# Last part of W2 gated by columns, x written into the PSUM banks ahead of its products, last norm read from PSUM

## The chip, the cores and the metric

The kernel runs on one core of one Trainium2 chip. The metric is the device time in microseconds (us) of one execution. A profiled execution has a span (first to last event in its trace) that is a little shorter than its device time. In the profile PE is TensorE's products, PEld its weight loads, DVE is VectorE, ACT is ScalarE, POOL is GpSimd, SP is SyncE, which issues the DMAs.

## The reference, cut to what matters

Two layers of a diffusion trunk over 640 tokens (128 context tokens and 512 latent tokens) with 1024 features. The change is in the second half of the last layer, whose MLP ends in a gated sum and a LayerNorm:

```python
def _layer_norm(x, g, b, eps=1e-5):
    mu = jnp.mean(xf, axis=-1, keepdims=True)
    var = jnp.mean(jnp.square(xf - mu), axis=-1, keepdims=True)
    y = (xf - mu) * lax.rsqrt(var + eps) * g + b

def _block(x, mod, mixer, g, b, w1, w2):
    sh1, sc1, gt1, sh2, sc2, gt2 = jnp.split(mod, 6, axis=-1)
    ...
    hf = x * (1 + sc2) + sh2
    ff = jnp.square(jax.nn.relu(hf @ w1)) @ w2
    x = _layer_norm(ALPHA * x + gt2 * ff, g[1], b[1])
```

The gate gt2 is one row of 1024 numbers for the context tokens and another for all latent tokens. So for the latent tokens gt2 * (h @ w2) may also be computed as h @ (w2 with its columns multiplied by gt2).

## The kernel before

The 640 tokens are five tiles t = 0 to 4 of 128; t = 0 is the context. x is kept in SBUF as two halves a = 0, 1 of 512 columns for each t. Every product of a weight W is made of three fp32r products: each weight unit `wraw` (128 rows, 1024 columns, 512 KB) is loaded by DMA into one of three slots (`NRAW`), then split by `Unit.split` into `whi`, a rounded copy made by ACT, and `wlo`, the rest made by DVE. Five split units fit at once (`NSPL`). An activation is split in the same way (`ghi`, `glo`).

The MLP goes in eight groups g of 512 hidden features. For g = 0 to 6, DVE collects the products of W2 in `y`; at g = 6, POOL multiplies `y` by the gate row and DVE adds it to ALPHA * x. For the last group, g = 7, `mlp_block(t, nh)` makes the product of tile t and column half nh in a PSUM bank `fps` (12 products of 512 columns over two units of W2), and `gated` has DVE multiply the bank by the gate row (`tmp`) and add it to x. After both halves of a tile, `norm` runs: DVE's `bn_stats` on both halves and `bn_aggr`, a square root on ACT, four small DVE operations that give `r` and `nmr`, and in the last layer the result itself. There a column range is done either by ACT (scale and shift by r and nmr), then two POOL operations (times the row ln_g, plus the row ln_b), or by two DVE operations (`stt`); `cut` says how many columns of tile t go the first way. Each finished range is written to `y` by a DMA from SP.

The order in which the engines get their instructions is set by a planner in the kernel (`class Order`): it advances a modelled clock, and where several steps could go next it takes the one that its own costs make ready first. Each engine's queue then runs strictly in that order; an instruction that waits holds all those behind it. `use(key)` makes sure that the units of a piece of W2 are split before its products, and `background` loads and splits units ahead when a slot is free. In the profile nearly all instructions have the line of a helper: L379 for DVE, ACT and POOL, L468 for products, L452 for DMAs, so that they are told apart by their tiles.

Of the kernel before, what the change touches and what calls it, by code (L numbers as in the profile page):

```python
# [13 lines left out]
ALU = mybir.AluOpType  # L14
# [392 lines left out]
def trunk_kernel(ctx: ExitStack, tc: tile.TileContext, io: dict, layers: int = 2, stop: str = ""):  # L407
# [105 lines left out]
    class Unit:  # L513


        def __init__(self, src, kt, n, own=False):
            self.src, self.kt, self.n, self.own = src, kt, n, own

        def load(self):
            tot = self.kt * self.n  # L520
# [4 lines left out]
        def split(self):  # L525
            tot = self.kt * self.n
            raw, self.raw = self.raw, None
            if self.own:

                self.hs, self.ls = [], []  # L530
                for k in range(0, self.kt, 2):
                    c = slice(k * self.n, min(k + 2, self.kt) * self.n)
                    w = c.stop - c.start
                    h, l_ = slot("whs")[:, :w].bitcast(F32R), slot("wls")[:, :w].bitcast(F32R)
                    act.copy(h, raw[:, c])
                    vec_tt(l_, raw[:, c], h.bitcast(F32), op=ALU.subtract)
# [12 lines left out]
            self.lo = lo[:, :tot].rearrange("p (k n) -> p k n", k=self.kt)  # L549
# [109 lines left out]
            yield 0.0  # L659

    done = set()
    pieces = {}
    units = []
    rank = {}
# [17 lines left out]
    for l in range(layers):  # L682
        if l == 1:
            add_piece((1, "SKVG"), [Unit(io["w_odd0"][:, 288 * a:288 * b], b - a, 288)
                                    for a, b in ((0, 3), (3, 6), (6, 8))])
            for n, kname in enumerate(ODD[1:]):
                add_piece((1, kname), [Unit(io["w_odd"][n, u], 4, 256) for u in range(2)])
        for h in range(2):
            for n in range(4):
                add_piece((l, "O", h, n), [Unit(io["w_out"][l, h, n], 4, 256)])  # L690
        for g in range(8):
            for n in range(2):
                add_piece((l, "1", 2 * g + n), [Unit(io["w_1"][l, 2 * g + n, u], 4, 256, g + n == 0) for u in range(2)])
            for n in range(2):
                add_piece((l, "2", g, n), [Unit(io["w_2"][l, g, n, u], 2, 512) for u in range(2)])
    pos = [0, 0, 0]
    mod_steps = []
    for c in range(6 if layers > 1 else 0):
# [230 lines left out]
    def norm(t, rows, ft, A, B, final, key, xd=None):  # L929
# [19 lines left out]
        time = order.step[:]  # L949
        if final:  # L950

            cut = (1024, 1024, 1024, 1024, 256)[t]
            for a, c0, c1 in ((0, 0, 256), (0, 256, 512), (1, 0, 512)) if t == NT - 1 else ((0, 0, 512), (1, 0, 512)):
                c, far = slice(c0, c1), 512 * a + c1 <= cut
                x, g, b = X[t][a][:, c], rows[0][a][:, c], rows[1][a][:, c]
# [7 lines left out]
                load(io["y"][t * P:(t + 1) * P, 512 * a + c.start:512 * a + c.stop], x)  # L963
            return
        def update():
            for a in range(2):
# [959 lines left out]
    def layer(l, ft, xd):  # L1926
# [34 lines left out]
        for g in range(8):  # L1961
# [14 lines left out]
            else:  # L1976
                if g == 6:
                    need_mods(l, (5,))
                    rows = gate_rows(l, 1)
                for f in range(4):  # L1980
                    sp = pss("ff") if f < 2 else None
                    for half in range(2):
# [9 lines left out]
                        squared(two(sp), *[two2(x) for x in (*parts[f], slot("relu2")[:, :TOK])])  # L1992

            def mlp_block(t, nh):
                w = use((l, "2", g, nh), (l, "2", g, 0) if last else None)
# [19 lines left out]
            else:  # L2015
                ln = ln_rows(l, 1)
                ft_n = A = B = None
                if not last_layer:
# [2 lines left out]
                    A, B = norm_cols(l, 1)  # L2021
                    ft_n = FT("h")
                xd = [[dram.tile([P, 512], F32, name=nm("xd")) for _ in range(2)] for _ in range(NT)]
                for t in range(NT):
                    for nh in range(2):
                        order.gemm(lambda: mlp_block(t, nh))
                    order.spawn(norm(t, ln, ft_n, A, B, last_layer, ("h", l, t), xd[t]))
        if last_layer:
            order.drain(lambda: not order.chains)
            return None, None  # L2030
# [114 lines left out]
```

## Time and profile before

| | us |
|---|---|
| median of three runs | 1635.65 (1634.84 to 1637.54) |
| the profiled execution | 1635.63 |
| its span | 1633.8 |
| PE busy | 1570.0 (96%) |
| DVE, ACT, POOL busy | 1018.0, 610.4, 524.7 |

The profiled execution is as long as the median. PE is busy nearly all the way, so a time is mostly a sum of products; the stretch that the change touches is the last 45 us, from the last group's first product with W2 at 1589.57 us of the span to its end.

### The profile page before, as it was taken

What the parts mean: (1) busy time and instruction counts of PE and PEld (TensorE: products, weight loads), DVE (VectorE), ACT (ScalarE), POOL (GpSimd) and SP (SyncE); (2) the same over time, 40 slices, a digit from 0 to 9 for tenths busy, and PEclk for the clock granted to TensorE, in tenths of its full rate; (3) what the DMA queues carried; (4) which work ended last, traced back from release to release, by engine and by line L of the source; (5) the groups of instructions that cost most, each with busy time, mean ns of one, the idle gap of its engine ahead of it and who ended that gap; (6) DMA issues with size and microseconds to landing.
All of it is one profiled execution on the core that took longest, in us unless ns stands there. A gap on an engine that the chain in (4) does not pass through costs nothing.

```text
span 1633.8 us, 28517 instructions
## 1 busy us (share of the span) xinstructions
PE 1570.0 (96%) x11345; PEld 1421.7 (87%) x11345; DVE 1018.0 (62%) x1943; ACT 610.4 (37%) x1279; POOL 524.7 (32%) x451
## 2 busy tenths in 40 slices
PE   7999999999999999999999998889999999999996
PEld 4998999999889889988988887779989988998994
DVE  3776662676477677676786788777824444444457
ACT  2554443336323222222255555553633222322321
POOL 2110000012467777777537347231200010011226
PEclk9999999999999999999999999999999999999998
DMA  9633334341444444463324101114212222223121
GB/s 333 204 119 118 102 98 162 130 134 52 139 136 143 148 139 152 147 182 114 112 68 139 61 28 39 56 43 155 79 52 78 78 78 72 71 75 113 58 78 65
DMA packets 89844, 177.75 MB, mean 109 GB/s; under 512 B 23648, under 2 KB 30832, under 8 KB 89712
## 3 DMA queue, kind: packets, MB, share of 16 engines
q1 hardware_dynamic: 89712, 175.94, 33.6%
q8 instruction: 89, 1.46, 0.4%
q14 instruction: 43, 0.35, 0.1%
HBM read 169.40 MB, written 6.50 MB: 108 GB/s over the span
## 4 chain that ended last, share of the span: by engine, by line
PE 80%; DVE 6%; ACT 5%; POOL 4%; DMA 2%; issue 2%; SPq 0%; POOLq 0%; DVEq 0%; ACTq 0%
PE ff L468 25%; PE fps L468 24%; PE proj L468 11%; PE ops L468 6%; PE fproj L468 3%; ACT h L379 1%; PE early L468 1%; DMA wmod<-in_w_mod 1%; POOL x L379 1%; PE sd L468 1%; PE po L468 1%; DVE wlo L379 1%; POOL y L379 1%; PE odp L468 1%; PE gl L468 1%
## 5 line engine op out<-in xcount | busy, mean ns | idle before, releaser
L468 PE MATMUL ff<-hh,whi 128*128 128x320 f32 (+2 forms) x960 | 297.2, 310 | 0.0
L468 PE MATMUL ff<-hh,wlo 128*128 128x320 f32 (+2 forms) x960 | 296.5, 309 | 0.1
L468 PE MATMUL ff<-hl,whi 128*128 128x320 f32 (+2 forms) x960 | 296.4, 309 | 0.0
L379 ACT CAST whi<-wraw 128x1024 fp32r<-128x1024 f32 (+1 forms) x183 | 189.3, 1045 | 285.4 <-PE fps L468 250.5
L379 DVE TENSOR_TENSOR wlo<-wraw,whi 128x1024 fp32r<-128x1024 f32 (+1 forms) x183 | 244.2, 1339 | 68.8 <-ACT whi L379 68.6
L468 PE MATMUL fps<-wlo,ghi 128*128 128x512 f32 (+1 forms) x648 | 253.9, 392 | 2.0 <-DVE wlo L379 2.0
L468 PE MATMUL fps<-whi,ghi 128*128 128x512 f32 (+1 forms) x648 | 254.5, 393 | 0.0
L468 PE MATMUL fps<-whi,glo 128*128 128x512 f32 (+1 forms) x648 | 253.5, 391 | 0.0
L379 POOL TENSOR_TENSOR x<-x,lnrow 128x512 f32<-128x512 f32 (+1 forms) x78 | 110.4, 1429 | 347.9 <-DVE y L379 216.7
L468 PEld LDWEIGHTS ff<-hh,whi 128*128 128x128 f32 x960 | 180.2, 188 | 3.1 <-issue 2.1
L379 DVE TENSOR_TENSOR relu<-relu 128x320 f32<-128x320 f32 (+3 forms) x100 | 64.1, 641 | 189.5 <-ACT ghi L379 185.9
L468 PEld LDWEIGHTS ff<-hl,whi 128*128 128x128 f32 x960 | 180.2, 188 | 0.6
L468 PEld LDWEIGHTS ff<-hh,wlo 128*128 128x128 f32 x960 | 180.2, 188 | 0.4 <-DVE wlo L379 0.4
L379 ACT ACTIVATE relu<-ff 128x320 f32<-128x320 f32 (+3 forms) x100 | 51.4, 514 | 295.2 <-PE ff L468 295.2
L379 DVE TENSOR_TENSOR y<-fps,y 128x512 f32<-128x512 f32 x120 | 82.6, 689 | 117.8 <-PE fps L468 117.7
L468 PEld LDWEIGHTS fps<-wlo,ghi 128*128 128x128 f32 x648 | 121.8, 188 | 29.9 <-DVE wlo L379 2.9
L468 PEld LDWEIGHTS fps<-whi,ghi 128*128 128x128 f32 x648 | 121.6, 188 | 29.6 <-issue 2.5
L468 PEld LDWEIGHTS fps<-whi,glo 128*128 128x128 f32 x648 | 121.7, 188 | 28.0
L379 POOL TENSOR_SCALAR wmod<-wmod,cs 128x512 f32<-128x512 f32 x84 | 95.2, 1134 | 124.1 <-DVE moda L379 108.5
L379 POOL TENSOR_TENSOR moda<-moda,wmod 128x512 f32<-128x512 f32 x84 | 123.5, 1470 | 6.2
L468 PE MATMUL ops<-wlo,cath 128*128 128x256 f32 x320 | 90.2, 282 | 2.2 <-DVE wlo L379 2.2
L468 PE MATMUL proj<-whi,hh 128*128 128x256 f32 (+1 forms) x280 | 83.9, 300 | 8.6 <-DVE sg L379 5.7
(295 smaller groups left out, 3372.2 us busy)
## 6 DMA issues: line engine op xcount, KB each, us to landing
wraw<-in_w SPq DMA_DIRECT2D x128, 512.0 KB
wmod<-in_w_mod SPq DMA_DIRECT2D x128, 256.0 KB
wmodp<-in_w_mod SPq DMA_DIRECT2D x64, 256.0 KB
wraw<-in_w_even SPq DMA_DIRECT2D x24, 512.0 KB
wraw<-in_w_out SPq DMA_DIRECT2D x16, 512.0 KB
wraw<-in_w_odd SPq DMA_DIRECT2D x16, 512.0 KB
gate<-mrow SPq DMA_DIRECT2D x16, 256.0 KB
xT<-in_xT SPq DMA_DIRECT2D x8, 320.0 KB
```

What stands on the lines that cost most here:

```text
L379: i = f(*a, **k)
L468: nc.tensor.matmul(o, a, b, **kw)
```

## The change

For the tiles t = 1 to 4 of the last layer's last group, four things are done otherwise. First, the four units of W2 for g = 7 are loaded once more (piece `"gated"`), and POOL multiplies each by the latent gate row, two operations of 128x512 per unit, before ACT and DVE split it. Tile 0 still goes the old way, through the ungated units and `gated`. Second, `preload` opens the PSUM bank of a block one block ahead: one product that starts the bank, and an ACT copy of x (128x512) into that bank over the result of the product; the 12 products of `whole_block` then add to what stands there. Third, the DVE multiply and add of `gated` are gone for these tiles, and `norm` reads the banks in place of x. Fourth, in the last norm half of the columns of t = 1 to 3 go to DVE's two operations (`cut` is 512 in place of 1024), and tile 4's last half is done in two ranges of 256.

```diff
@@ Unit.split
+            if self.gate is not None:
+                for k in range(self.kt):
+                    c = slice(k * self.n, (k + 1) * self.n)
+                    pool.tensor_tensor(raw[:, c], raw[:, c], last_gates[self.gate][:, :self.n], op=ALU.mult)
...
@@ the list of units
+    for n in range(2):
+        add_piece(("gated", n), [Unit(io["w_2"][layers - 1, 7, n, u], 2, 512, gate=n) for u in range(2)])
...
@@ norm
-            dve.bn_stats(st[:, i, :], X[t][a][:, c0:c1])
+            dve.bn_stats(st[:, i, :], source(a, c0, c1))
...
-            cut = (1024, 1024, 1024, 1024, 256)[t]
+            cut = (1024, 512, 512, 512, 256)[t]
...
-                    act.activation(x, x, AF.Identity, scale=r, bias=nmr)
+                    act.activation(x, y, AF.Identity, scale=r, bias=nmr)
...
-                    stt(x, x, mv[:, 0:1], g, op0=ALU.subtract, op1=ALU.mult)
+                    stt(x, y, mv[:, 0:1], g, op0=ALU.subtract, op1=ALU.mult)
...
@@ layer
+                def preload():
+                    if todo:
+                        t, a, c0, c1 = todo.pop(0)
+                        ps = (acc if t in (1, 3) or c0 else pss)("out", True)
+                        banks.setdefault(t, {})[a, c0, c1] = ps
+
+                        hv = parts[0][0]
+                        mm(ps[:, :c1 - c0], hv[:, :128], hv[:, :c1 - c0], start=True, stop=False)
+                        act.copy(ps[:, :c1 - c0], X[t][a][:, c0:c1])
+
+                def whole_block(t, a, c0, c1):
+                    preload()
+                    w = use(("gated", a), ("gated", 0))
+                    c, n, ps = tcol(t), slice(c0, c1), banks[t][a, c0, c1][:, :c1 - c0]
+                    for f in range(4):
+                        hv, lv = parts[f]
+                        mm(ps, hv[:, c], w.hi(f, n), start=False, stop=False)
+                        mm(ps, hv[:, c], w.lo(f, n), start=False, stop=False)
+                        mm(ps, lv[:, c], w.hi(f, n), start=False, stop=(f == 3))
```

What the planner makes of it is seen in the queues. On POOL, behind the last product of `y` and the gate (`y_14079`), there stood before only the last norm. x_12786 and x_13014 are the halves of tile 0, x_12831 and x_13048 those of tile 1:

```order
L379 TENSOR_TENSOR y_14079<-y_14079,gate_16313 128x512
L379 TENSOR_TENSOR x_12786<-x_12786,lnrow_17011 128x512
L379 TENSOR_TENSOR x_13014<-x_13014,lnrow_17013 128x512
L379 TENSOR_TENSOR x_12786<-x_12786,lnrow_17015 128x512
L379 TENSOR_TENSOR x_13014<-x_13014,lnrow_17017 128x512
L379 TENSOR_TENSOR x_12831<-x_12831,lnrow_17011 128x512
```

Now, at the same place on POOL, wraw_16951 and wraw_16983 are the gated units of the left half (the first and the second unit), wraw_17078 and wraw_17131 those of the right half (the third and the fourth):

```order
L379 TENSOR_TENSOR y_14079<-y_14079,gate_16313 128x512
L379 TENSOR_TENSOR wraw_16951<-wraw_16951,gate_16311 128x512 x2
L379 TENSOR_TENSOR wraw_16983<-wraw_16983,gate_16311 128x512 x2
L379 TENSOR_TENSOR wraw_17078<-wraw_17078,gate_16313 128x512 x2
L379 TENSOR_TENSOR x_12786<-x_12786,lnrow_17015 128x512
L379 TENSOR_TENSOR x_13014<-x_13014,lnrow_17017 128x512
L379 TENSOR_TENSOR x_12786<-x_12786,lnrow_17019 128x512
L379 TENSOR_TENSOR x_13014<-x_13014,lnrow_17021 128x512
L379 TENSOR_TENSOR wraw_17131<-wraw_17131,gate_16313 128x512 x2
L379 TENSOR_TENSOR x_12831<-x_12831,lnrow_17015 128x512
```

Three units are gated ahead of tile 0's norm and the fourth behind it; tiles 1 to 3 have two POOL operations each in place of four.

On ACT, behind the split of the last ungated unit (whi_17049), there now stand copies of x into banks (out_17053 and out_17080 for tile 1, out_17133 and out_17177 for tile 2), the splits of the gated units (whi_17074, whi_17085, whi_17127, whi_17138, in the order of POOL above), and tile 0's norm between them:

```order
L379 CAST whi_17049<-wraw_16852 128x1024
L379 COPY out_17053<-x_12831 128x512
L379 COPY out_17080<-x_13048 128x512
L379 CAST whi_17074<-wraw_16951 128x1024
L379 CAST whi_17085<-wraw_16983 128x1024
L379 COPY out_17133<-x_12879 128x512
L379 ACTIVATE sq_17107<-mv_17102,eps_t 128x1
L379 ACTIVATE x_12786<-x_12786,nmr_17110,r_17109 128x512
L379 ACTIVATE x_13014<-x_13014,nmr_17110,r_17109 128x512
L379 CAST whi_17127<-wraw_17078 128x1024
L379 CAST whi_17138<-wraw_17131 128x1024
L379 COPY out_17177<-x_13082 128x512
```

Before, the same split of the last ungated unit was followed by the norms alone, one square root and two scalings for each tile:

```order
L379 CAST whi_17045<-wraw_16852 128x1024
L379 ACTIVATE sq_17087<-mv_17082,eps_t 128x1
L379 ACTIVATE x_12786<-x_12786,nmr_17090,r_17089 128x512
L379 ACTIVATE x_13014<-x_13014,nmr_17090,r_17089 128x512
L379 ACTIVATE sq_17143<-mv_17138,eps_t 128x1
```

On DVE, behind the sum of tile 0's right half (x_13014), the queue is now the rest of the left half's gated units, the whole norm of tile 0 up to nmr, the rest of the right half's units, and then tile 1's norm, which reads the banks:

```order
L379 TENSOR_TENSOR x_13014<-x_13014,tmp_17069 128x512
L379 TENSOR_TENSOR wlo_17075<-wraw_16951,whi_17074 128x1024
L379 TENSOR_TENSOR wlo_17086<-wraw_16983,whi_17085 128x1024
L379 BN_STATS bn_17101<-x_12786 128x6
L379 BN_STATS bn_17101<-x_13014 128x6
L379 BN_AGGR mv_17102<-bn_17101 128x2
L379 TENSOR_SCALAR veh_17106<-mv_17102 128x1
L379 RECIPROCAL sq_17107<-sq_17107 128x1
L379 TENSOR_SCALAR q_17108<-sq_17107,veh_17106 128x1
L379 TENSOR_SCALAR r_17109<-q_17108,sq_17107 128x1
L379 TENSOR_SCALAR nmr_17110<-mv_17102,r_17109 128x1
L379 TENSOR_TENSOR wlo_17128<-wraw_17078,whi_17127 128x1024
```

The two sums of tile 1's halves, which stood among these rows before, are gone. On PE the product that opens out_17080 stands directly behind tile 0's right half, and the one that opens out_17133 behind tile 1's left half. Up to the last group's products the queues of PE, DVE, ACT and POOL are as before; on SP two of the four added loads stand ahead of the last norm's rows, and two behind.

## Rows read from the trace of the kernel before

**Rows 1.** The page's first part, the engines over the whole span.
```profile
span 1633.8 us, 28517 instructions
PE 1570.0 (96%) x11345; PEld 1421.7 (87%) x11345; DVE 1018.0 (62%) x1943; ACT 610.4 (37%) x1279; POOL 524.7 (32%) x451
```

**Rows 2.** The chain that ended last, 1500 us on: start us, length us, what.
```profile
1533.82 27.74 PE fps L468 x120
...
1595.17 12.53 PE fps L468 x53
...
1611.63 18.63 POOL x L379 x13
```

**Rows 3.** Timeline of PE: start us, length us, operation [idle before it, released by].
```profile
1595.17 0.50 PE L468 MATMUL fps<-wlo,ghi 128*128 128x512 f32 x1 [1.02 <-DVE wlo L379]
...
1596.19 0.40 PE L468 MATMUL fps<-whi,glo 128*128 128x512 f32 x1
...
1618.55 0.28 PE L468 MATMUL fps<-whi,glo 128*128 128x256 f32 x1
```

**Rows 4.** Timeline of DVE, columns as for PE.
```profile
1597.96 0.69 DVE L379 BATCH_NORM_STATS2 bn<-x 128x6 f32<-128x512 f32 x1
...
1603.51 0.27 DVE L379 TENSOR_SCALAR q<-sq,veh 128x1 f32<-128x1 f32 x1
...
1604.06 0.21 DVE L379 TENSOR_SCALAR nmr<-mv,r 128x1 f32<-128x1 f32 x1
...
1618.87 0.42 DVE L379 TENSOR_TENSOR tmp<-fps,gate 128x256 f32<-128x256 f32 x1
...
1622.68 0.26 DVE L379 BATCH_NORM_AGGREGATE mv<-bn 128x2 f32<-128x24 f32 x1
1622.98 0.74 DVE L379 SCALAR_TENSOR_TENSOR x<-x,mv,lnrow 128x256 f32<-128x256 f32 x1
...
1625.99 2.47 DVE L379 SCALAR_TENSOR_TENSOR x<-x,r,lnrow 128x256 f32<-128x256 f32 x2
```

**Rows 5.** Timeline of ACT, columns as for PE.
```profile
1590.67 1.04 ACT L379 CAST whi<-wraw 128x1024 fp32r<-128x1024 f32 x1
1601.44 0.30 ACT L379 ACTIVATE sq<-mv,eps_t 128x1 f32<-128x1 f32 x1 [9.72 <-DVE mv L379]
1604.31 1.52 ACT L379 ACTIVATE x<-x,nmr,r 128x512 f32<-128x512 f32 x2 [2.58 <-DVE nmr L379]
```

**Rows 6.** ACT's groups over the whole span: count, busy us, mean ns, idle before.
```profile
L379 ACT CAST hh<-h 128x512 fp32r<-128x512 f32 x30 | 18.9, 629 | 0.5
L379 ACT COPY y<-fps 128x512 f32<-128x512 f32 x20 | 11.8, 588 | 35.0 <-PE fps L468 35.0
```

**Rows 7.** Timeline of POOL, columns as for PE.
```profile
1541.08 2.15 POOL L379 TENSOR_TENSOR y<-y,gate 128x512 f32<-128x512 f32 x1 [1.46 <-issue]
1544.63 1.29 POOL L379 TENSOR_TENSOR y<-y,gate 128x512 f32<-128x512 f32 x1 [1.40 <-DVE y L379]
...
1611.63 19.43 POOL L379 TENSOR_TENSOR x<-x,lnrow 128x512 f32<-128x512 f32 x14 [0.46 <-ACT x L379]
```

**Rows 8.** Timeline of DVE at two splits in earlier stretches.
```profile
1522.89 1.22 DVE L379 TENSOR_TENSOR wlo<-wraw,whi 128x1024 fp32r<-128x1024 f32 x1
...
1540.86 1.22 DVE L379 TENSOR_TENSOR wlo<-wraw,whi 128x1024 fp32r<-128x1024 f32 x1
```

**Rows 9.** Windows: stretch, length, engines' busy us (instructions), granted clock, DMA share, GB/s.
```profile
1526.50:1527.00 0.50, 0.50 (x5) 0.50 (x5) 0.00 (x0) 0.12 (x1) 0.00 (x0) 1.00 0.43 172
1527.00:1527.50 0.50, 0.50 (x6) 0.50 (x4) 0.00 (x0) 0.47 (x2) 0.00 (x0) 1.00 0.08 8
```

**Rows 10.** PE after a long wait in the middle of the kernel, timeline.
```profile
1059.27 0.55 PE L468 MATMUL proj<-whi,hh 128*128 128x256 f32 x1 [5.66 <-DVE sg L379]
```

**Rows 11.** Windows around that wait, columns as in the other windows.
```profile
1060.00:1063.00 3.00, 3.00 (x16) 3.00 (x15) 0.37 (x2) 3.00 (x9) 2.28 (x3) 0.50 0.00 0
1063.00:1064.00 1.00, 1.00 (x9) 1.00 (x7) 0.11 (x1) 0.07 (x1) 1.00 (x2) 0.76 0.00 0
```

More of the change, by code (lines that the diff above doesn't have):

```diff
@@ L513, in trunk_kernel, with __init__ @@
     class Unit:
-        def __init__(self, src, kt, n, own=False):
-            self.src, self.kt, self.n, self.own = src, kt, n, own
+        def __init__(self, src, kt, n, own=False, gate=None):
+            self.src, self.kt, self.n, self.own, self.gate = src, kt, n, own, gate
         def load(self):
@@ L661, in trunk_kernel @@
     done = set()
+    last_gates = []
     pieces = {}
@@ L927, in summed, with norm, source @@
             stt(x, x, ALPHA, y, op0=ALU.mult, op1=ALU.add)
-    def norm(t, rows, ft, A, B, final, key, xd=None):
+    def norm(t, rows, ft, A, B, final, key, xd=None, banks=None):
+        def source(a, c0, c1):
+            for (h, b0, b1), ps in (banks or {}).items():
+                if h == a and b0 <= c0 and c1 <= b1:
+                    return ps[:, c0 - b0:c1 - b0]
+            return X[t][a][:, c0:c1]
         cuts = [(0, 0, 512), (1, 0, 512)] if t < NT - 1 else [(0, 0, 256), (0, 256, 512), (1, 0, 256), (1, 256, 512)]
@@ L950, in norm @@
         if final:
-            cut = (1024, 1024, 1024, 1024, 256)[t]
-            for a, c0, c1 in ((0, 0, 256), (0, 256, 512), (1, 0, 512)) if t == NT - 1 else ((0, 0, 512), (1, 0, 512)):
+            cut = (1024, 512, 512, 512, 256)[t]
+            for a, c0, c1 in ((0, 0, 256), (0, 256, 512), (1, 0, 256), (1, 256, 512)) if t == NT - 1 \
+                    else ((0, 0, 512), (1, 0, 512)):
                 c, far = slice(c0, c1), 512 * a + c1 <= cut
-                x, g, b = X[t][a][:, c], rows[0][a][:, c], rows[1][a][:, c]
+                x, g, b, y = X[t][a][:, c], rows[0][a][:, c], rows[1][a][:, c], source(a, c0, c1)
                 if far:
-                    act.activation(x, x, AF.Identity, scale=r, bias=nmr)
+                    act.activation(x, y, AF.Identity, scale=r, bias=nmr)
                     pool.tensor_tensor(x, x, g, op=ALU.mult)
@@ L960, in norm @@
                 else:
-                    stt(x, x, mv[:, 0:1], g, op0=ALU.subtract, op1=ALU.mult)
+                    stt(x, y, mv[:, 0:1], g, op0=ALU.subtract, op1=ALU.mult)
                     stt(x, x, r, b, op0=ALU.mult, op1=ALU.add)
                 load(io["y"][t * P:(t + 1) * P, 512 * a + c.start:512 * a + c.stop], x)
+            for ps in (banks or {}).values():
+                order.release(ps)
             return
@@ L1979, in layer @@
                     rows = gate_rows(l, 1)
+                    if last_layer:
+                        last_gates.extend(rows[0])
                 for f in range(4):
@@ L1994, in mlp_block @@
             def mlp_block(t, nh):
-                w = use((l, "2", g, nh), (l, "2", g, 0) if last else None)
+                w = use((l, "2", g, nh), (l, "2", g, 0) if last and not last_layer else None)
                 c = tcol(t)
@@ L2023, in layer, with step @@
                 xd = [[dram.tile([P, 512], F32, name=nm("xd")) for _ in range(2)] for _ in range(NT)]
-                for t in range(NT):
-                    for nh in range(2):
-                        order.gemm(lambda: mlp_block(t, nh))
-                    order.spawn(norm(t, ln, ft_n, A, B, last_layer, ("h", l, t), xd[t]))
+                todo = [(t, a, 256 * i, 256 * j) for t in range(1, NT) for a in range(2)
+                        for i, j in (((0, 1), (1, 2)) if t == NT - 1 and a else ((0, 2),))] if last_layer else []
+                banks = {}
+                def preload():
[15 more added lines that the diff above has]
+                        mm(ps, lv[:, c], w.hi(f, n), start=False, stop=(f == 3))
+                blocks = todo[:]
+                for t in range(NT):
+                    if last_layer and t:
+                        for b in blocks:
+                            if b[0] == t:
+                                order.gemm(lambda: whole_block(*b))
+                    else:
+                        for nh in range(2):
+                            def step():
+                                if nh:
+                                    preload()
+                                mlp_block(t, nh)
+                            order.gemm(step)
+                    order.spawn(norm(t, ln, ft_n, A, B, last_layer, ("h", l, t), xd[t], banks.get(t)))
         if last_layer:
```

## The prediction

> **What bounds the kernel now.** I read the page first: PE is busy for 96% of the span [rows 1], so time can only be won where PE waits or where the kernel runs on after PE. The chain of waits names both places in the last stretch [rows 2]. One is a wait of 1.02 us inside tile 0's right half, for the split of the last ungated unit [rows 3]. The other is the tail: PE's last product starts at 1618.55 us and lasts 0.28 [rows 3], and the span ends at 1633.8 [rows 1], 15.0 us later. In that tail the chain is POOL, which does 14 operations of the norm without a gap from 1611.63 to 1631.06, and 2.74 us for the last transfer and the end [rows 7]. So the change can win at most the tail, if it doesn't hold PE up in exchange. PE stands at full clock and has 120 products of 512 columns in 27.74 us, 2.77 us for a block of 12 and 0.23 for one product [rows 2].
>
> **What is removed and added, by engine.** DVE loses the multiply and the add for seven blocks of 512 columns and two of 256, and gains four splits and six operations of the norm: about even. POOL loses six operations of the norm and gains eight to gate W2. PE gains nine opening products: seven at 0.23 and two at 0.12, 1.85 us in all. ACT gains nine copies into banks and four splits. SP gains four loads of 512 KB. In sums nothing here is too much; what decides is where the new operations stand in the queues, since each queue runs in order. So I follow the chain from the last point that is as before, with prices from rows.
>
> **The prices.** A split costs 1.04 on ACT [rows 5], then 1.22 on DVE [rows 8]. A POOL operation of 128x512 costs 1.29 alone [rows 7] and 19.43 over 13 (twelve and two of half width) = 1.49 in the busy tail; I take 1.40. A root is 0.30, two scalings of 512 are 1.52 [rows 5], statistics of 512 are 0.69, and from q to the end of nmr it is 4 short steps in 0.76 (1603.51 to 1604.27) [rows 4]. No row shows an ACT copy into PSUM. The nearest are a copy out of PSUM, 0.59, and a cast in SBUF, 0.63 [rows 6]; I take 0.59, as the forms are alike, and at the other end it adds under 0.1 to the chain. DVE read of a bank at the price of the SBUF form: the statistics' 0.69 is used. A load: the slot of a split that ended at 1524.11 [rows 8] was loaded again by about 1527.0 [rows 9], so 3 us from free slot to data. The gated units' first three loads follow splits that end by 1595.13, so their data is there by 1598.1, and POOL, with nothing else in front of them in its queue, has gated the first two long before and the third by 1600.9. All that is hidden: nobody asks for the third before 1606. On SP the norm's rows ln_g and ln_b now stand behind two of these loads; they are asked for first at 1605, more than 10 us after those loads were issued. The fourth load needs the slot of the first gated unit and lands about 1602.5, also hidden, for a reason that comes now.
>
> **The chain.** Up to 1595.17 nothing moves. Tile 0's right half ends on PE at 1596.59 [rows 3]; the bank opener before it hides in the 1.02 wait. Only then does PE open the bank for tile 1's right half (until 1596.8). ACT's copy into this bank stands ahead of the splits of the first two gated units, so that they wait for it: copy to 1597.4, splits to 1599.4, DVE's second rest to 1600.7. PE's left half of tile 1, which waits for these, ends at 1602.3. That is a new wait of 2.8 us on PE (three pieces: whi, wlo of the first unit, wlo of the second), since without it this block would have been issued by 1599.4.
>
> Next, ACT's copy for tile 2 waits for an opener that stands on PE behind tile 1's left half: opener to 1602.5, copy to 1603.15. Behind this copy stands tile 0's root (to 1603.45; DVE's statistics for it are ready by 1602.4). Reciprocal and the steps to nmr end at 1604.4, tile 0's two scalings at 1605.2 and 1605.95, and only behind these does ACT split the third gated unit, to 1607.0. PE has issued the opener and has waited since 1602.3: **4.7 us idle** in front of tile 1's right half.
>
> Half of that block needs the fourth unit. On POOL its gating stands behind tile 0's four operations of the norm, and these can't start before ACT's first scaling ends: four times 1.40 from 1605.2 is 1610.85, the gating two times 1.40, to 1613.65, the split on ACT to 1614.7, the rest on DVE to 1615.9. PE does its six products and waits again, **some 5 us** in two pieces (4.2 for whi, 0.7 for wlo). All later blocks have both halves' units and their banks are filled in time: per tile PE needs 5.5 us and DVE 4, so no wait is due there.
>
> From 1615.9 PE has five products (1.16), six blocks (16.6) and six openers (1.16): 1634.8. To this comes the clock. In the middle of the kernel PE waited 5.66 us [rows 10], and from its restart at 1059.27 the granted clock was 0.50, the 1.2 GHz level, and back at 2.4 GHz about 1063.5 [rows 11]. So 4.2 us at half the clock cost up to 2.1. Here the first 0.7 of it falls on PE's last wait, so I take 1.4, with 0 and 2.1 as bounds. The restart after the first long wait costs nothing more, as its six products are followed by a wait anyway. PE's last result is there at 1636.5, 17.7 us later than before.
>
> The tail gets shorter. After the last product DVE does statistics of 256 columns (0.42, as the 256-wide read of a bank [rows 4]), the aggregate 0.26 [rows 4], two subtractions and the reciprocal (1.0), 0.76 to nmr, and four operations of 256. These cost 0.74 to 0.82 with POOL busy all along [rows 4, 7], and I take 0.45, since POOL has only two operations of 256 left, which wait for ACT's scaling. DVE ends at 1640.9 and POOL, with 0.6 on ACT and twice 0.75 behind nmr, at 1641.3; they touch each other, so 1641.5. With the 2.74 of the end the span is 1644.2. The profiled execution was 1635.63 for a span of 1633.8 [rows 1], 1.83 around it, and it stands at the median of the runs, 1635.65. So I forecast **1646.0 us**, 10.4 more than before (0.64%).
>
> One rule bears on the price of POOL and of the tail. A POOL operation that ran into a DVE split took 2.15 us and its neighbour without one 1.29 [rows 7, 8]. The Trainium skill (SBUF — State Buffer, section "SBUF: two separate sides") says that VectorE with two SBUF inputs and GpSimd share a pair of ports as a lock: whoever comes first holds it for the whole instruction, the other waits. By that rule, and the trace agrees (0.86 of waiting beside a split of 1.22), tile 0's four operations cost 1.29 each and meet one split, 6.0 where I have 5.6, the gating meets none, 2.6 where I have 2.8, and the sum would be 1646.2.
>
> **Rivals.** First, faster after all: the two long waits don't come, because the fourth unit's gating and both right-half splits are through when PE asks. Then PE goes on at 1602.3 with an opener, a block, six blocks and six openers, to 1622.9, the tail of 5.0 and 2.74 follows, and the span is 1630.7: 1632.5 us, 0.2% faster. Without the wait for the left half too it is 1629.7. It decides itself at the two long waits: the new tail is 7.3 us shorter, and the openers and the first wait take 4.2 of that, so more than 3 us of further waiting on PE eats the gain. For it speaks the 15 us of tail to be won; against it the three queues, in which tile 0's norm stands ahead of the third unit's split and the fourth unit's gating. Between this and the forecast lies no change: one of the two waits hidden, 1632.5 plus about 4.
>
> Second, the clock stays low. The 18.9 us of products after 1615.9 would then all run at half, some 17.5 more than the 1.4 taken: 1662. Against it, the restart in rows 11 was back at full clock while PE worked on.
>
> Third, POOL is slower. If each of the six operations in the chain meets a DVE operation, they cost 2.15, +4.5 us: 1650.5. Against it, DVE stands still for most of 1605 to 1614. This belongs to the forecast's upper end, as does a tail at the dearer price of DVE's operations, +1.5. At the low end are no clock loss (-1.4), POOL at 1.29 (-0.7) and a tail without contact (-0.5): 1643.4.
>
> **Numbers.** The forecast with its bounds 0.86, the low clock 0.04; no change 0.05; faster 0.05. A difference under 0.2% can hardly be told from none here: the three runs of before lie 0.17% apart. The range runs from 1641.5, a little under the low end, as some steps may overlap by more than I see, to 1652, the upper end with both dear prices. Slower by over 0.2% holds 0.90.
>
> **What would show it.** In the profile after, PE's row should show an idle of 4 to 5 us ahead of the first product of tile 1's right half, released by ACT's whi, and one of about 4 in the middle of this block, also by whi; the granted clock falls to 0.50 for some us around 1607 to 1618. POOL's gating of the fourth unit starts about 1611. PE's last product ends about 1636.5, and the tail after it is 7 to 8 us in place of 15.0. If PE ends before 1625, the queues didn't hold it and the first rival is true; if the waits stand there but the sum of them is under 6 us, tile 0's norm was quicker than I have it.

## The result, and the profile after

The changed kernel takes 1649.3 us (median of four runs, 1646.58 to 1651.06) where the kernel before takes 1636.6 on the same chip (four runs, 1634.84 to 1637.93): a ratio of 1.0077, with a 95% interval of 1.0059 to 1.0095. It is 12.7 us slower; the forecast was 1646.0 in a range of 1641.5 to 1652.0. The profiled execution took 1648.94 us for a span of 1647.2.

The page's first part, as in [rows 1]:

```profile
span 1647.2 us, 28571 instructions
PE 1579.4 (96%) x11354; PEld 1425.6 (87%) x11354; DVE 1021.6 (62%) x1937; ACT 616.5 (37%) x1289; POOL 525.9 (32%) x453
```

PE is busy 9.4 us longer than before for nine products more, where the prediction has 1.85 for them, so part of its products took longer. The other 4.0 of the 13.4 us of span are idle time: more waits in front of products, less a tail behind PE that is 7.3 shorter. The timeline of PE shows where (start us, length us, operation, idle before it and what released it); the first row here is the one that began at 1595.17 in [rows 3]:

```profile
1595.71 0.50 PE L468 MATMUL fps<-wlo,ghi 128*128 128x512 f32 x1 [0.80 <-DVE wlo L379]
1596.98 0.40 PE L468 MATMUL out<-ghi 128*128 128x512 f32 x1
1599.04 0.50 PE L468 MATMUL out<-whi,ghi 128*128 128x512 f32 x1 [1.65 <-ACT whi L379]
1600.29 0.50 PE L468 MATMUL out<-wlo,ghi 128*128 128x512 f32 x1 [0.76 <-DVE wlo L379]
1602.53 0.50 PE L468 MATMUL out<-wlo,ghi 128*128 128x512 f32 x1 [0.57 <-DVE wlo L379]
...
1608.59 0.79 PE L468 MATMUL out<-whi,ghi 128*128 128x512 f32 x1 [4.40 <-ACT whi L379]
1610.61 0.80 PE L468 MATMUL out<-wlo,ghi 128*128 128x512 f32 x1 [1.23 <-DVE wlo L379]
1616.50 0.79 PE L468 MATMUL out<-whi,ghi 128*128 128x512 f32 x1 [3.38 <-ACT whi L379]
1617.76 0.79 PE L468 MATMUL out<-wlo,ghi 128*128 128x512 f32 x1 [0.47 <-DVE wlo L379]
...
1639.24 0.28 PE L468 MATMUL out<-whi,glo 128*128 128x256 f32 x1
```

From the opener at 1596.98 to 1617.76 PE waits 12.5 us: 3.0 in front of and in tile 1's left half, 5.6 in front of its right half and behind that half's first product, 3.9 in the middle of it. The last result is there at 1639.52, and the span ends 7.7 us later, where it was 15.0 before. The last operations of the norm in that tail are POOL's:

```profile
1642.74 1.59 POOL L379 TENSOR_TENSOR x<-x,lnrow 128x256 f32<-128x256 f32 x2 [2.83 <-ACT x L379]
```

The queues of ACT and POOL say why the two long waits stand where they do:

```profile
1604.23 0.59 ACT L379 COPY out<-x 128x512 f32<-128x512 f32 x1 [4.30 <-PE out L468]
1604.76 0.29 ACT L379 ACTIVATE sq<-mv,eps_t 128x1 f32<-128x1 f32 x1
1606.09 1.52 ACT L379 ACTIVATE x<-x,nmr,r 128x512 f32<-128x512 f32 x2 [1.04 <-DVE nmr L379]
1607.51 1.03 ACT L379 CAST whi<-wraw 128x1024 fp32r<-128x1024 f32 x1
1615.40 1.04 ACT L379 CAST whi<-wraw 128x1024 fp32r<-128x1024 f32 x1 [6.86 <-POOL wraw L379]
```

```profile
1599.15 4.46 POOL L379 TENSOR_TENSOR wraw<-wraw,gate 128x512 f32<-128x512 f32 x2 [9.25 <-DMA wraw<-in_w]
1606.98 5.95 POOL L379 TENSOR_TENSOR x<-x,lnrow 128x512 f32<-128x512 f32 x4 [3.36 <-ACT x L379]
1612.89 2.48 POOL L379 TENSOR_TENSOR wraw<-wraw,gate 128x512 f32<-128x512 f32 x2
```

The third unit's data is gated at 1603.6 and waits 3.9 us for ACT, which does the copy, tile 0's root and its two scalings first. The fourth unit's gating begins only when POOL is through with tile 0's four operations. DVE's splits, in the same stretch:

```profile
1599.01 3.46 DVE L379 TENSOR_TENSOR wlo<-wraw,whi 128x1024 fp32r<-128x1024 f32 x2 [0.41 <-ACT whi L379]
...
1608.57 1.99 DVE L379 TENSOR_TENSOR wlo<-wraw,whi 128x1024 fp32r<-128x1024 f32 x1 [2.52 <-ACT whi L379]
1616.48 1.23 DVE L379 TENSOR_TENSOR wlo<-wraw,whi 128x1024 fp32r<-128x1024 f32 x1 [5.92 <-ACT whi L379]
```

Of the first two, which run beside POOL's gating of the third unit, one takes 1.22 (from 1599.01) and the next 2.31 (from 1600.16); the third, beside tile 0's operations on POOL, takes 1.99; the last, with POOL idle, takes 1.23, as in [rows 8]. The windows (columns as in [rows 9]) show the clock:

```profile
1606.00:1607.00 1.00, 0.00 (x0) 0.00 (x0) 0.05 (x1) 0.91 (x2) 0.02 (x1) 0.56 0.00 0
...
1618.00:1623.00 5.00, 5.00 (x12) 3.88 (x13) 2.84 (x10) 0.84 (x2) 0.00 (x0) 0.50 0.02 3
1623.00:1624.00 1.00, 1.00 (x5) 0.82 (x4) 0.62 (x1) 0.65 (x1) 0.00 (x0) 0.91 0.03 8
```

It falls to the 1.2 GHz level in the first long wait and is back at 2.4 GHz only at 1623.1, over 5 us after PE's last wait. From 1617.76 to the opener at 1624.52 PE has 18 products, 4.2 us at the 0.23 of [rows 2]; they took 6.76, so the clock costs 2.6 us there.

### The profile page after: what moved, and what is told of

Its sections match the earlier page's. It is cut to its first block, busy times and chain, and to the rows that moved or that the text cites. A ratio compares the mean times of both kernels' runs of the same rounds, so it can differ in the third digit from the quotient of the medians.

```text
span 1647.2 us, 28571 instructions
## 1 busy us (share of the span) xinstructions
PE 1579.4 (96%) x11354; PEld 1425.6 (87%) x11354; DVE 1021.6 (62%) x1937; ACT 616.5 (37%) x1289; POOL 525.9 (32%) x453
## 4 chain that ended last, share of the span: by engine, by line
PE 82%; DVE 6%; ACT 4%; DMA 3%; issue 2%; POOL 2%; SPq 0%; POOLq 0%; ACTq 0%; DVEq 0%
PE ff L468 26%; PE fps L468 24%; PE proj L468 10%; PE ops L468 6%; PE fproj L468 3%; DMA wmod<-in_w_mod 1%; PE early L468 1%; ACT h L379 1%; PE out L468 1%; PE sd L468 1%; DVE wlo L379 1%; PE po L468 1%; PE odp L468 1%; PE gl L468 1%; PE ss L468 1%
## 5 line engine op out<-in xcount | busy, mean ns | idle before, releaser
L379 ACT CAST whi<-wraw 128x1024 fp32r<-128x1024 f32 (+1 forms) x187 | 193.3, 1045 | 293.2 <-PE fps L468 237.9
L379 DVE TENSOR_TENSOR wlo<-wraw,whi 128x1024 fp32r<-128x1024 f32 (+1 forms) x187 | 251.5, 1350 | 78.8 <-ACT whi L379 78.6
L468 PE MATMUL fps<-wlo,ghi 128*128 128x512 f32 (+1 forms) x612 | 240.6, 393 | 1.8 <-DVE wlo L379 1.8
L468 PE MATMUL fps<-whi,ghi 128*128 128x512 f32 (+1 forms) x612 | 241.4, 394 | 0.2 <-DVE y L379 0.2
L468 PE MATMUL fps<-whi,glo 128*128 128x512 f32 (+1 forms) x612 | 240.2, 392 | 0.0
L379 POOL TENSOR_TENSOR x<-x,lnrow 128x512 f32<-128x512 f32 (+1 forms) x72 | 100.4, 1402 | 332.0 <-DVE y L379 217.3
L468 PEld LDWEIGHTS fps<-whi,ghi 128*128 128x128 f32 x612 | 114.9, 188 | 29.0 <-issue 2.5
L468 PEld LDWEIGHTS fps<-wlo,ghi 128*128 128x128 f32 x612 | 115.0, 188 | 28.3 <-DVE wlo L379 2.7
L468 PEld LDWEIGHTS fps<-whi,glo 128*128 128x128 f32 x612 | 114.9, 188 | 26.9
L468 PE MATMUL proj<-whi,h0h 128*128 128x256 f32 x320 | 91.6, 286 | 0.1
```

The costliest lines, as they stand in the source:

```text
L379: i = f(*a, **k)
L468: nc.tensor.matmul(o, a, b, **kw)
```

## The experiments

Theory: the added work is cheap, but the three in-order queues put tile 0's norm ahead of the third unit's split (ACT) and of the fourth unit's gating (POOL); what PE loses there, and the clock behind it, is more than the shorter tail gives. Rivals: the added work costs as such, wherever it stands; the clock is the whole loss; the new split of columns in the norm alone would have won the tail. Each kernel's ratio is against runs of the kernel before on the same chip. Executions differ ahead of the changed stretch: the product that follows PE's wait in tile 0's right half (1595.71 above) begins between 1594.4 and 1597.5 in them, so that parts are compared from that product on. In the profiled executions, one of each kernel, the whole stretch from the first product behind those of the last group with W1 (1589.57 before, 1590.11 changed) to the end of the span takes, in us: before 44.2, changed 57.1, e1 48.3, e2 56.8, e3 51.6, e4 55.7, e5 44.0, e6 47.6, e7 47.9, e8 44.6, e9 45.3, e10 42.5, e11 42.4.

**Tile 0's norm later (e1).**

```diff
+                    if last_layer and t == 0:
+                        continue
+                    if last_layer and t == 1:
+                        order.spawn(norm(0, ln, ft_n, A, B, True, ("h", l, 0)))
                     order.spawn(norm(t, ln, ft_n, A, B, last_layer, ("h", l, t), xd[t], banks.get(t)))
```

> Only the order is changed: tile 0's norm is given to the planner behind tile 1's blocks, with all added work kept. On POOL the fourth gating now stands ahead of tile 0's four operations, on ACT both right-half splits stand ahead of tile 0's root and scalings. The theory (PE waits because the in-order queues put tile 0's norm first): the third unit is split by about 1607.1 us of the span and the fourth by 1609.2, in place of 1610.6 and 1617.7; PE's long waits shrink from 4.4 and 3.4 us to under 2 each, the clock stays up, PE's last result comes near 1628.4 in place of 1639.5, and with a tail of 7.7 and 1.75 around the span the time is 1638 (1637 to 1641, the upper end if the clock still falls). The rival (the added loads, gating, openers and copies cost as such, wherever they stand): the time stays at 1647 to 1649.

1639.45 us, ratio 1.0017 (1.0005 to 1.0029). PE's waits in the last stretch (engine, what was waited for, us in total, times, longest), and POOL's timeline:

```profile
PE out L468 <- ACT whi L379: 3.3, 2, 1.7
PE out L468 <- DVE wlo L379: 1.5, 2, 0.8
```

```profile
1598.97 6.76 POOL L379 TENSOR_TENSOR wraw<-wraw,gate 128x512 f32<-128x512 f32 x4 [9.67 <-DMA wraw<-in_w]
1616.64 10.95 POOL L379 TENSOR_TENSOR x<-x,lnrow 128x512 f32<-128x512 f32 x8 [10.90 <-ACT x L379]
```

All four gatings stand together now, and the wait in the middle of tile 1's right half is gone. The same operations in another order lose 2.4 us in place of 12.7: some ten of the 12.7 us are the order (8.8 of 12.9 by the stretches above), and the rival falls for these. One part of the expectation was missed: the clock fell all the same, twice for 3.4 us, behind the waits of 1.7 and 0.8 that are left in front of and in both halves of tile 1, and PE's last result came at 1630.57 in place of 1628.4.

**Third gating shrunk (e2).** `pool_as_512` is POOL with the planner's price of 512 columns:

```diff
+                    if self is pieces["gated", 1].units[0]:
+                        c = slice(k * self.n, k * self.n + 16)
+                        pool_as_512.tensor_tensor(raw[:, c], raw[:, c], last_gates[self.gate][:, :16], op=ALU.mult)
+                        continue
```

> The gating of the third unit covers 16 columns in place of 512 in each of its two operations, the planner being told the old price, so that every queue has the same order as in the changed kernel; the rest of that unit stays ungated. The theory that this gating, which runs on POOL beside DVE's two wlo of the left half, stretches them (3.46 us for the pair, 1.22 for one alone): the pair takes 2.4 to 2.5, PE starts tile 1's right half 1.1 us earlier (about 1607.5 in place of 1608.6) and everything behind it too, 1648.2 in all. The rival (the gating is hidden, as predicted, and the pair is slow for another reason): the pair stays at 3.4 and the time at 1649.3. The times alone can hardly tell 1.1 us; the two rows of DVE and PE do.

1649.09 us, ratio 1.0074 (1.0057 to 1.0091), as the changed kernel. DVE's pair, and the clock in the left half's end:

```profile
1599.58 2.38 DVE L379 TENSOR_TENSOR wlo<-wraw,whi 128x1024 fp32r<-128x1024 f32 x2 [0.42 <-ACT whi L379]
```

```profile
1604.00:1606.00 2.00, 1.38 (x4) 0.56 (x2) 0.00 (x0) 0.59 (x2) 0.00 (x0) 0.64 0.00 0
```

The pair takes 2.38 in place of 3.46 and PE's wait of 0.57 is gone: that the gating stretches DVE's splits is shown. The gain in time was missed. In this execution the clock fell at 1602.0, inside tile 1's left half, which in the changed kernel's profile ran at full clock, so the block ended 8.7 us behind the product that follows the wait in tile 0's right half, in place of 8.3. What the collision is worth in time stays open; it is too small for these medians, and the stretch is 0.3 shorter only.

**Fourth unit not gated (e3).**

```diff
-            if self.gate is not None:
+            if self.gate is not None and self is not pieces["gated", 1].units[1]:
```

> The fourth unit isn't gated at all, so that its split doesn't wait for POOL; everything else stands in the same order, the other three units are gated. It removes 2.5 us of POOL's work. The theory (the fourth unit is late because its gating stands behind tile 0's four operations on POOL): ACT splits it straight behind the third, by 1609.6 us, DVE by 1612.6, so the wait of 3.4 and 0.5 in the middle of tile 1's right half is gone, its eighth product starts near 1612.8 in place of 1617.8, the half clock covers fewer products behind it, and the time is 1643.4 (1642.5 to 1645). The rival (the cost is the added work as such): 1648 to 1649.3.

1642.59 us, ratio 1.0038 (1.0025 to 1.0051). PE's eighth product of tile 1's right half comes without a wait in front of it:

```profile
1613.14 0.63 PE L468 MATMUL out<-wlo,ghi 128*128 128x512 f32 x1
```

Taking 2.5 us of work from an engine that is busy a third of the span wins 6.7. With e1, where that work stays and only moves, this says that it is its place that counts.

**Waits filled (e4).** In the block of tile 1's right half; `fill` is a bank that nobody reads, `hf` a part of the activation:

```diff
                     for f in range(4):
                         hv, lv = parts[f]
+                        for _ in range({0: 17, 2: 15}.get(f, 0) if fill is not None else 0):
+                            nc.tensor.matmul(fill, hf[:, :128], hf[:, :512], start=True, stop=True)
```

> Added products of 128x512 into a bank that nobody reads fill PE's two long waits: 17 ahead of the first product of tile 1's right half and 15 ahead of the seventh, at 0.23 each 3.9 and 3.5 us. Queues of the other engines keep their order. The theory that the clock falls because PE stands still, and that this costs 2.6 us behind the second wait: the granted clock stays 1.0, the products behind 1617.8 come 0.23 apart in place of 0.43, and the time is 1646.7 (1646.3 to 1647.5; a little is lost where fillers overrun a wait). The rival (the clock falls all the same, since other waits or something else lower it): the fillers cost 0.43 each, 13.8 in all, overrun both waits by about 6 us together, and the time is 1653 to 1656.

1646.7 us, ratio 1.0056 (1.0041 to 1.0071), as the theory has it. PE's timeline:

```profile
1604.39 4.05 PE L2067 MATMUL fill<-ghi 128*128 128x512 f32 x17
...
1618.21 0.50 PE L468 MATMUL out<-wlo,ghi 128*128 128x512 f32 x1 [0.56 <-DVE wlo L379]
...
1622.48 0.39 PE L468 MATMUL out<-ghi 128*128 128x512 f32 x1
```

The 18 products from 1618.21 to 1622.48 take 4.27 us, not 6.76: the 2.5 us of the clock come back. Half of the expectation was too simple: the clock still fell twice, from 1600.8 to 1604.2 in tile 1's left half and from 1611.0 to 1614.4 behind the unfilled wait of 1.55; the second stretch costs nothing, since the split that PE needs next was later anyway. The first makes tile 1's left half 1.0 longer than in the changed kernel's profile, where the clock did not fall there, so that the stretch is only 1.4 shorter. The clock behind the second long wait is 2.5 of 12.7 us and not the whole loss.

**The split of columns alone, in the kernel before (e5).**

```diff
-            cut = (1024, 1024, 1024, 1024, 256)[t]
+            cut = (1024, 512, 512, 512, 256)[t]
```

(and tile 4's last half in two ranges).

> The kernel before with the last norm's new split of columns alone (half of the columns of tiles 1 to 3 on DVE, tile 4's last half in two ranges of 256), and nothing else of the change: no added loads, gating on POOL, openers or copies; PE's products are as before. POOL loses six operations, DVE gains six of 0.75 us and one short one. The theory that the shorter tail needs DVE to be freed from the gating: DVE is without a gap from about 1602 us to 1628.5 already, the 4.5 to 4.9 us more are given back in part where it doesn't run into POOL (0.9, 0.9, 0.6 and the like in the rows of before), so DVE becomes the end of the chain at 1629 to 1631 and the time is 1635 (1633.5 to 1637). The rival (the tail is won by the columns alone): a tail of 7.7 us behind PE's last product as in the changed kernel, 1628.5.

1636.06 us, ratio 0.9997 (0.9987 to 1.0006): no change, inside the expected range, and the rival falls. PE's last product starts at 1620.15, POOL's last two operations at 1630.79, behind DVE's nmr at 1629.86:

```profile
1629.86 0.21 DVE L379 TENSOR_SCALAR nmr<-mv,r 128x1 f32<-128x1 f32 x1
```

```profile
1630.79 1.85 POOL L379 TENSOR_TENSOR x<-x,lnrow 128x256 f32<-128x256 f32 x2 [1.94 <-ACT x L379]
```

The tail is POOL's in the kernel before, until 1631.06 [rows 7], but DVE ends only 2.6 us sooner, at 1628.46 [rows 4]; what is taken from POOL here, DVE takes up. In the changed kernel, where DVE loses the gating of the banks too, the tail is 7.7; a kernel that takes the gating from DVE alone was not run.

**And the left units early (e6).** With e1's edit, and in tile 0's right half's step, ahead of its products:

```diff
                                 if nh:
                                     preload()
+                                    if last_layer:
+                                        use((l, "2", g, 1), (l, "2", g, 1))
+                                        while pos[0] <= rank[id(pieces["gated", 0].units[-1])]:
+                                            split_unit()
```

> As the run with tile 0's norm behind tile 1's blocks, and the first two gated units are split ahead of tile 0's right half's products, so that ACT does them before it waits for the bank opener behind that half. The theory: the wait of 3 us ahead of and in tile 1's left half is gone (1.65, 0.76 and less), this block ends by 1600.2 us; then the third unit, gated from 1599 on, becomes the one that is late: PE waits for it until about 1602.7 and 1603.9, the fourth costs under 1.5 more, so 2.5 to 4 of it are kept: 1636.3 (1635 to 1638). The rival (the wait only moves to the third and fourth units, whose load sets the time): 1639 to 1639.5, as in that run.

1638.16 us, ratio 1.0013 (1.0005 to 1.0021), just outside the range and hardly better than e1. On ACT only the first of the two left units' splits got ahead of the copy that waits for PE (at 1593.74), the second stands behind it (1597.82). The opener behind tile 1's left half comes at 1601.44, 3.1 us sooner than in e1, counted from the product behind tile 0's wait; but PE then waits 1.79 for the third unit and 1.23 for DVE's rests, and 6.8 us run at half clock:

```profile
1603.63 0.50 PE L468 MATMUL out<-whi,ghi 128*128 128x512 f32 x1 [1.79 <-ACT whi L379]
```

Most of the gain moved on into the next waits, as the rival has it.

**Left halves first (e7).** With e6's early splits, the blocks in a new order, and tile 0's norm given to the planner behind the third left half:

```diff
+                todo = [(t, a, 0, 512) for a in range(2) for t in range(1, NT - 1)] if last_layer else []
+                todo += [(NT - 1, 0, 0, 512), (NT - 1, 1, 0, 256), (NT - 1, 1, 256, 512)] if last_layer else []
...
```

> As the run before it, and the blocks go in another order: the left halves of tiles 1, 2 and 3, then the right halves of 1, 2 and 3, then tile 4; tiles 2 and 3 use the two banks of one tile each; tile 0's norm is given to the planner behind the third left half. The right units are then asked for 5.9 us later. The theory: no wait over 1 us stands on PE behind tile 0, the clock stays at 1.0, PE's last result comes at 1621 to 1622 (1596.9 + 8 blocks of 2.77 + openers 1.7), DVE has the norms of tiles 1 to 3 close together and may end up to 2 us later than PE allows, tail 7.7 to 9.7: span 1628.7 to 1631.5, 1631.5 (1630 to 1633.5), faster than before by 0.2 to 0.4%. The rival (openers, copies and gating cost PE as such, or DVE is the bound): 1636 or more, no gain over before.

1639.96 us, ratio 1.0028 (1.0019 to 1.0037): 8.5 us above the forecast, and slower than before. ACT's timeline, and PE's:

```profile
1608.97 0.81 ACT L379 ACTIVATE x<-x,nmr,r 128x512 f32<-128x512 f32 x1 [1.04 <-DVE nmr L379]
1609.68 1.03 ACT L379 CAST whi<-wraw 128x1024 fp32r<-128x1024 f32 x1
```

```profile
1610.77 0.69 PE L468 MATMUL out<-whi,ghi 128*128 128x512 f32 x1 [2.30 <-ACT whi L379]
```

The planner put the fourth split between tile 0's two scalings, behind a copy that waited for PE. It was gated by 1605.2; PE waited for it until 1610.8, and 6.8 us at half clock followed. The same fault, in a new place.

**Banks early (e8), and tile 1 on POOL (e9).** With e7's order of blocks:

```diff
+                ahead = {(2, 0): 2, (3, 0): 2, (3, 1): 1, (4, 0): 1, (4, 1): 1}
+
                 def whole_block(t, a, c0, c1):
-                    preload()
+                    preload(ahead.get((t, a), 0))
...
+                                if b[:2] == (2, 0):
+                                    use(("gated", 1), ("gated", 0))
```

e9 besides has `cut` = (1024, 1024, 512, 512, 256).

> As the run with the left halves first, with two corrections of order: the fourth gated unit's split is asked for one block sooner (behind tile 2's left half), so that ACT has it ahead of tile 0's root and scalings, and the banks are opened in other places (tile 1's left half ahead of tile 0's left half, tile 2's ahead of tile 0's right half, the right halves two blocks ahead), so that ACT's copies don't hold the splits. Same operations in all. The theory (what was left in that run were the two waits of 2.3 and 0.8 us ahead of and in tile 1's right half, for a split that stood behind tile 0's scaling, and the 6.5 us at half clock behind them): both waits go, the clock stays at 1.0, PE's last result comes 25 to 26 us behind the product that follows tile 0's last wait (33.2 in that run), DVE keeps up, the tail is 7.7 to 9, the time 1631 to 1633.5, 0.2 to 0.3% faster than before. The rival (DVE, with the norms of tiles 1 to 3 close together, is the bound): PE ends early, but the tail is 10 or more, 1635 to 1637, no gain.

> As the run beside it, with all columns of tile 1 done by ACT and POOL in the last norm (two POOL operations more, two of DVE's less), which moves 1.5 us from DVE to POOL. If DVE is the bound of the tail there, this one is up to 1.5 us faster; if PE is, the two are the same within 0.1%; if POOL becomes the bound, it is slower by up to 2.

1636.36 us, ratio 1.0002 (0.9994 to 1.0011), and 1636.39, ratio 1.0001 (0.9992 to 1.0010): both as before. In e8 PE keeps full clock to its last product, and its last result is there 27.6 us behind the product at 1597.50, as expected save for two waits of 1.0. But the tail is 11.2 (PE, POOL and DVE in turn):

```profile
1624.86 0.28 PE L468 MATMUL out<-whi,glo 128*128 128x256 f32 x1
```

```profile
1616.37 13.92 POOL L379 TENSOR_TENSOR x<-x,lnrow 128x512 f32<-128x512 f32 x10 [9.94 <-ACT x L379]
```

```profile
1627.75 1.41 DVE L379 BATCH_NORM_STATS2 bn<-out 128x6 f32<-128x256 f32 x4
```

The rival with DVE as the bound is true here: DVE comes to tile 4's statistics 2.6 us after PE's end, and POOL had stood idle for 9.9 us. One of PE's waits, 0.96 for ACT's copy into the other half of a two-bank tile, was new. In e9 POOL works from 1614.74 for 17.5 us without a gap, to 1632.3, and DVE ends at 1632.6; the tail is 11.9, and what DVE is spared there, POOL takes up.

**Tile 0's norm between (e10), and tile 1 on POOL again (e11).** On top of e8 and e9; tile 0's norm is no longer given behind tile 3's left half:

```diff
-                ahead = {(2, 0): 2, (3, 0): 2, (3, 1): 1, (4, 0): 1, (4, 1): 1}
+                ahead = {(2, 0): 2, (3, 0): 1, (1, 1): 1, (3, 1): 1, (4, 0): 1, (4, 1): 1}
...
                                 if b[:2] == (2, 0):
                                     use(("gated", 1), ("gated", 0))
+                                    order.spawn(norm(0, ln, None, A, B, True, ("h", l, 0)), 0.0)
```

> As the run with the left halves first and the banks early, with two moves: tile 0's norm is given to the planner one block sooner, behind tile 2's left half, so that DVE does its statistics while it waits for the right units' splits and POOL starts its four operations straight behind the gating; and each bank is opened only when the other half of the same PSUM tile has its products behind it. The theory (there DVE and POOL were the bound: PE's last result at 1625.1, but DVE still at work on the norms until 1632.9 and POOL until 1633.5, since POOL stood idle for 9.9 us before tile 0's operations): POOL's idle goes, DVE is through with tile 3 by 1624 to 1625 in that run's time, the tail is 7.7 to 8.5, the time 1632 to 1633.5, 0.15 to 0.25% faster than before. The rival (the order on DVE doesn't matter, DVE's sum is the bound): 1635.5 to 1636.5.

> As the run beside it, with all columns of tile 1 done by ACT and POOL in the last norm, which takes 1.5 us from DVE and gives 2.7 to POOL. If DVE is still the bound there, this one is 0.5 to 1.5 us faster; if it is PE with its tail of 7.7, they are the same; if POOL becomes the bound, up to 2 slower.

e10: 1634.84 us, ratio 0.9988 (0.9979 to 0.9997), between the theory's 1632 to 1633.5 and the rival's 1635.5: POOL starts tile 0's operations after 4.2 us of idle time in place of 9.9, but the tail is 10.2 where 7.7 to 8.5 was expected, since DVE still comes to tile 4's statistics 1.7 us after PE's last result.

```profile
1609.63 5.17 POOL L379 TENSOR_TENSOR x<-x,lnrow 128x512 f32<-128x512 f32 x4 [4.19 <-ACT x L379]
```

e11: 1633.87 us, ratio 0.9983 (0.9975 to 0.9992). In e11 PE has one wait of 1.0 behind tile 0, no product at half clock, and POOL, which was the tail of 19 us in [rows 7], is through with tiles 0 to 3 2.8 us after PE's last result (1621.25):

```profile
PE out L468 <- DVE wlo L379: 1.0, 1, 1.0
```

```profile
1607.87 16.14 POOL L379 TENSOR_TENSOR x<-x,lnrow 128x512 f32<-128x512 f32 x12 [4.19 <-ACT x L379]
```

So the change can win, if little: 0.12% in place of 0.77% lost with its own operations in another order, an interval that just leaves out no change, and 0.17% with tile 1's columns back on ACT and POOL. That the second step itself gains is not shown: the two intervals overlap, and the stretches take 42.5 and 42.4. The tail is still 10.0, with DVE behind.

## Why the prediction was right

**The waits.** All three came where they were put, each begun by a wait for whi. The first was 3.0 (predicted 2.8), the second 4.40 and 1.23 (4.7, with DVE's rest not counted), the third 3.38 and 0.47 (some 5). The third is shorter because the six products ahead of it, at half clock and with DVE's rest of 1.99 behind the first, took 4.5 us (1608.59 to 1613.12), where the predicted sum leaves them 3.5. That costs nothing, as the fourth unit's split sets the pace there: POOL's four operations and the gating took 8.4, as predicted. e1 and e3 show that the cause of the two long waits is the order in the queues. The first wait was not taken away by itself; with one of the left units' splits ahead of ACT's copy (e6), and with both (e8), 1.0 of it was left.

**The tail.** 7.7 us, as predicted; DVE's reads of a bank and ACT's copies into one (0.59) cost what was taken.

**What was mis-sized.** The predicted span was 1644.2, that of the profile 1647.2. Of the 3.0 us, 0.5 is the stretch ahead of the change (1595.71 for 1595.17), and nearly all the rest is two terms. First, "All that is hidden" was wrong of the third unit's gating: it runs beside DVE's two rests of the left half (3.46 in place of 2.4), so that the left half ended 1.1 later than the sum had it; e2 shows the stretching, not its worth in time. Second, the clock: 1.4 was taken, with 2.1 as the upper bound, from a restart in mid-kernel that was back after 4.2 us [rows 11]. Here it was back 17.1 us after it fell and cost 2.6, 1.2 more; e4 gives 2.5 back. The bound was too low, since one recovery was taken for the rule; here the six products between the two long waits didn't bring the clock back, nor did the first five us behind them. Both terms lie on the same side, and the range held them because of the dear prices at its upper end, neither of which came.

**The rivals.** The way to a gain was named rightly: it decides itself at the two long waits. With both gone (e8) the forecast of that rival, 1632.5, still wasn't reached, since it took the tail of 5.0 and 2.74 for granted; with PE early, DVE and POOL are the tail, and it took two further moves (e10, e11) to come near. The low clock for good and the slower POOL didn't come. Two slips in the working change nothing: the low clock's 17.5 on top of the forecast makes 1663.5, not 1662, and from q to the end of nmr there are three steps in 0.76, not four.

## What to carry to other kernels

When work is moved from one engine to others, its sum on them says little: write down each queue in order and ask what stands ahead of the operation that the busiest engine waits for. Here the same operations cost 12.7 us or win 0.9 (e10), by the place of one norm, of a few splits and bank openers, and by the order of the blocks. A long wait on TensorE is to be priced with the half clock behind it (2.6 us here), and a tail that is cut on one engine is worth only the distance to the next engine behind it.

## What the runs showed of the hardware

**The clock** (granted clock, by windows of half a microsecond).

```profile
1600.50:1601.00 0.50, 0.50 (x3) 0.35 (x2) 0.50 (x1) 0.00 (x0) 0.50 (x1) 0.67 0.35 66
1604.00:1604.50 0.50, 0.50 (x3) 0.20 (x1) 0.00 (x0) 0.00 (x0) 0.50 (x2) 0.92 0.00 0
```

```profile
1600.50:1601.00 0.50, 0.50 (x3) 0.41 (x3) 0.50 (x1) 0.00 (x0) 0.50 (x1) 1.00 0.00 0
```

In e1 to e4 (e1's windows first, then the changed kernel's) it fell inside tile 1's left half while PE was at work again, 0.7 to 1.3 us after the product that followed a wait of 0.76 and, one product earlier, of 1.65; it stayed at the 1.2 GHz level for 3.4 us of nearly unbroken products. In the changed kernel's own profile the same waits brought no fall. Later stretches at half clock lasted 3.4 us (e1, e4), 6.8 (e3, e6, e7), 13.7 (e2) and 17.1 (the changed kernel); the last two have the wait of 3.4 in them. Why the same pattern of waits sometimes costs the clock and sometimes not stays open.

**DVE and POOL.** In the changed kernel DVE's first rest of the left half takes 1.22 (from 1599.01), and POOL's first gating beside it (from 1599.15) 2.23, where a gating alone took 1.24. Then DVE's second rest takes 2.31 (from 1600.16) and POOL's second gating 2.27: each that comes second is 1.0 to 1.1 longer. In e2 POOL's two operations of 16 columns took 2.38 together, as long as the two splits on DVE beside them, which cost no more than alone: POOL waits there, not DVE. The two gatings and two splits of the changed kernel share 1599.01 to 1603.61, 4.6 us, near the sum of their lengths alone (twice 1.24, the fourth's gating, and twice 1.19, e2's splits: 4.9). The Trainium skill (SBUF — State Buffer, section "SBUF: two separate sides") says that a DVE operation with two SBUF inputs and a GpSimd operation that reads SBUF share ports as a lock for a whole instruction, and the trace agrees with these numbers.
